# Up products of a ConvGLU feed-forward by one level of Strassen's algorithm, down products in pairs

## The chip, the cores and the metric

The kernel runs on one core of one Trainium2 chip. Its time is the device time of one launch in microseconds, the median of several runs. PE is TensorE, DVE is VectorE, ACT is ScalarE, POOL is GpSimd, and SP is SyncE, whose queue issues the transfers.

## The reference

One encoder layer runs over 2304 tokens of width 1024: 2048 of a sample and 256 of a prompt, with shared weights. After the mixers and the cross-attention comes the part that changes, and then the final norm:

```
a, g = split(rmsnorm(x) @ w_up)          # 1024 -> 2 x 2816: values a, gates g
g = conv over 3 neighbouring tokens of g, by channel, + bias
x = x + (silu(g) * a) @ w_down           # 2816 -> 1024
y = rmsnorm(x)
```

The convolution doesn't reach across the border of sample and prompt. Everything is float32.

## The kernel before

Products of float32 are made of two parts: hi is a value rounded to PE's format fp32r, lo the rest. `mm3` (lines 120 to 125) multiplies hi by hi, hi by lo and lo by hi into one PSUM tile. `load_split` (line 97) loads weights into a raw buffer, and ACT makes hi of them (line 116) and POOL lo (line 117).

`Ffn.run` works on three groups of 768 tokens (SG), each in two halves of 384 (TG). The 2816 inner features are 22 blocks f of 128. For each f, `up_part` loads the gates' and the values' weights and, half by half, adds 8 x 3 matmuls into `pg` (386 columns, the neighbours of the half with them) and 8 x 3 into `pa` (384 columns). Then comes the gate: ACT takes the middle tap of the convolution from `pg` (line 1958), DVE adds the outer two (line 1968), ACT makes tanh (line 1971), DVE two steps of the product (lines 1972 and 1973, the second with `pa`), ACT hi and POOL lo of the result u (lines 1975 and 1976).

`down_part` multiplies u of several f by their down weights: parts of 3, 3, 3, 3, 3, 3, 2, 2 blocks (PARTS). For each of 6 token blocks of 128 and each half of the 1024 outputs, 3 matmuls per f of 512 columns go into one `pd`, and DVE adds it to `acc` (line 1994). The last part also makes the output norm: a square on ACT (line 2000), a root on DVE, a scaling on ACT (line 2004), and a product with the weights of 1024 columns on POOL (line 2005).

`prep` makes the tokens of one half: it loads x, scales it by its norm (`rms_scale`, line 171), and transposes it on PE, and ACT and DVE make hi and lo of each transposed tile (`transpose_split`, lines 164 to 167), eight steps. `start` does this for the first half beside the last attention group, and the second is woven into the first up parts. For the next group it is woven into the last down parts.

PE's order is that of the code (`manual_schedule`). The order of the other engines' queues is made by the compiler's scheduler, which dispatches by readiness and, among ready ones, by the order of the code.

## Time and profile before

| | |
|---|---|
| median of 3 runs | 3730.86 us (3726.14 to 3733.28) |
| the profiled execution | 3726.75 us |
| its span | 3724.7 us |
| mean granted clock of PE | 0.981 |
| PE, DVE, ACT, POOL busy | 96%, 49%, 34%, 35% of the span |
| bytes moved | 340.37 MB, 91 GB/s on the mean |

The profile is one execution. Its span is what the engines' records cover, and the execution's own time is 2 us more. Durations of matmuls overlap, so what one costs is read from the distance of two starts.

### The profile page before, as it was taken

The numbers are of one execution on the slowest core, as the hardware profiler recorded it, in microseconds if no ns is written. First come the engines' busy times: TensorE is split into PE (matmuls) and PEld (weight loads), VectorE is DVE, ScalarE is ACT, GpSimd is POOL, SyncE is SP. The second block draws the span as 40 slices with busy tenths as digits, with TensorE's granted clock in tenths as the row PEclk, the third lists the DMA queues.
The fourth block names the chain that finished last, engine by engine and source line by source line (L and its number), as shares of the span: only waits on it lengthen the run. The fifth ranks groups of instructions, "written<-read, shape, count | busy, mean of one in ns | idle before, by whom it ended". The sixth has DMA issues, their size and how long they took to land.

```text
span 3724.7 us, 53214 instructions
## 1 busy us (share of the span) xinstructions
PE 3581.3 (96%) x20150; PEld 3084.8 (83%) x20150; DVE 1822.1 (49%) x4422; ACT 1275.4 (34%) x2632; POOL 1301.0 (35%) x1110
## 2 busy tenths in 40 slices
PE   7998999999899999999998999999999999999998
PEld 6998998898445555678887999988999998999997
DVE  5757777565653644355555333326333336333334
ACT  3321114453345445444444222224322224322222
POOL 3326435343345244200001433433423333433342
PEclk9999999999799999999998999999999999999999
DMA  6453443333141411312224212214211223211221
GB/s 209 165 190 110 164 151 105 108 125 83 44 122 45 118 38 27 129 52 75 74 74 154 74 52 68 74 62 134 87 52 57 68 75 101 87 57 52 63 80 51
DMA packets 212833, 340.37 MB, mean 91 GB/s; under 512 B 82913, under 2 KB 155105, under 8 KB 208353
## 3 DMA queue, kind: packets, MB, share of 16 engines
q1 hardware_dynamic: 212576, 336.97, 28.6%
q8 instruction: 159, 2.61, 0.3%
q14 instruction: 98, 0.79, 0.1%
HBM read 252.14 MB, written 84.77 MB: 90 GB/s over the span
## 4 chain that ended last, share of the span: by engine, by line
PE 83%; DVE 8%; DMA 3%; issue 2%; ACT 2%; POOL 1%; SPq 0%; ACTq 0%; DVEq 0%; POOLq 0%
PE pg L123 5%; PE pa L123 5%; PE pa L124 5%; PE pa L125 5%; PE pg L124 5%; PE pg L125 5%; PE pd L123 5%; PE pd L125 5%; PE pd L124 5%; PE po L1498 4%; PE mm L123 3%; PE mm L125 3%; PE mm L124 3%; PE ps L123 2%; PE pa L691 2%; PE ps L124 2%
## 5 line engine op out<-in xcount | busy, mean ns | idle before, releaser
L1968 DVE SCALAR_TENSOR_TENSOR gc<-pg,f_cw,gc 128x384 f32<-128x384 f32 (+4 forms) x308 | 166.5, 558 | 563.2 <-ACT gc L1958 559.4
L117 POOL TENSOR_TENSOR ul<-raw,uh 128x1024 fp32r<-128x1024 f32 x132 | 317.6, 2406 | 209.3 <-ACT uh L116 206.3
L123 PE MATMUL pg<-h,uh 128*128 128x386 f32 x1056 | 358.7, 340 | 0.9 <-DVE x L1809 0.9
L124 PE MATMUL pg<-h,uh 128*128 128x386 f32 x1056 | 357.6, 339 | 0.0
L125 PE MATMUL pg<-h,ul 128*128 128x386 f32 x1056 | 357.0, 338 | 0.0
L123 PE MATMUL pa<-h,uh 128*128 128x384 f32 x1056 | 356.9, 338 | 0.0
L124 PE MATMUL pa<-h,uh 128*128 128x384 f32 x1056 | 356.5, 338 | 0.0
L125 PE MATMUL pa<-h,ul 128*128 128x384 f32 x1056 | 356.3, 337 | 0.0
L1994 DVE TENSOR_TENSOR acc<-acc,pd 128x512 f32<-128x512 f32 x264 | 181.4, 687 | 312.9 <-PE pd L125 312.8
L123 PE MATMUL pd<-dh,uh 128*128 128x512 f32 x792 | 316.4, 399 | 8.1 <-DVE h L166 5.5
L1976 POOL TENSOR_TENSOR ul<-gc,uh 128x384 fp32r<-128x384 f32 x132 | 134.8, 1021 | 541.1 <-ACT uh L1975 541.1
L125 PE MATMUL pd<-dh,ul 128*128 128x512 f32 x792 | 313.8, 396 | 0.0
L124 PE MATMUL pd<-dl,uh 128*128 128x512 f32 x792 | 313.7, 396 | 0.0
L1481 POOL TENSOR_TENSOR sum<-sum,pe 128x512 f32<-128x512 f32 x168 | 214.2, 1284 | 194.6 <-ACT pe L1473 188.5
L117 POOL TENSOR_TENSOR dl<-raw,dh 128x1024 fp32r<-128x1024 f32 x66 | 158.8, 2406 | 265.1 <-ACT dh L116 265.1
L1958 ACT ACTIVATE gc<-pg,f_cw 128x384 f32<-128x384 f32 x132 | 87.2, 661 | 419.0 <-PE pg L125 415.8
L123 PE MATMUL mm<-wh,hhi 128*128 128x256 f32 x720 | 212.7, 295 | 4.6 <-DVE ut L363 4.0
L1473 ACT ACTIVATE pe<-ps 128x512 f32<-128x512 f32 (+1 forms) x264 | 151.0, 590 | 188.2 <-PE ps L1471 185.5
L123 PE MATMUL mm<-hhi,wh 128*128 128x384 f32 x576 | 208.0, 361 | 0.0
L1432 DVE TENSOR_REDUCE mx<-pm 128x1 f32<-128x512 f32 (+1 forms) x264 | 170.7, 678 | 72.0 <-PE pm L1429 70.9
L124 PE MATMUL mm<-wl,hhi 128*128 128x256 f32 x720 | 205.0, 285 | 0.0
L125 PE MATMUL mm<-wh,hlo 128*128 128x256 f32 x720 | 204.8, 284 | 0.0
(491 smaller groups left out, 8704.2 us busy)
## 6 DMA issues: line engine op xcount, KB each, us to landing
raw<-in_w_up SPq DMA_DIRECT2D x132, 512.0 KB
raw<-in_w_down SPq DMA_DIRECT2D x66, 512.0 KB
x<-in_x SPq DMA_DIRECT2D x36, 512.0 KB
hhi<-s_h SPq DMA_DIRECT2D x8, 1536.0 KB
hlo<-s_h SPq DMA_DIRECT2D x8, 1536.0 KB
raw<-in_w_in SPq DMA_DIRECT2D x22, 512.0 KB
s_h<-hhi SPq DMA_DIRECT2D x6, 1536.0 KB
s_h<-hlo SPq DMA_DIRECT2D x6, 1536.0 KB
```

The source lines that it names most:

```text
L117: (eng or nc.gpsimd).tensor_tensor(out=l, in0=raw, in1=f32(h), op=ALU.subtract)
L123: mm(out, lhsT=lh, rhs=rh, start=first, stop=False)
L124: mm(out, lhsT=lh, rhs=rl, start=False, stop=False)
L125: mm(out, lhsT=ll, rhs=rh, start=False, stop=last)
L1432: nc.vector.tensor_reduce(out=mx[:, qb, i:i + 1], in_=pm[:, :half], axis=AX.X, op=ALU.max)
L1473: nc.scalar.activation(out=pe[:, :nq], in_=ps[:, :nq], func=AF.Exp)
L1481: eng.tensor_tensor(out=t[:, :nq], in0=self.sums[h][:, :nq], in1=pe[:, :nq], op=ALU.add)
L1498: nc.tensor.matmul(po[hs, :nq], lhsT=va[:, vt, :], rhs=pe[:, :nq], start=kb == 0, stop=self.done)
L1958: nc.scalar.activation(out=gc, in_=pg[:, 1:TG + 1], func=AF.Identity, scale=cw[:, f, 1:2], bias=cw[:, f, 3:4])
L1968: V.scalar_tensor_tensor(out=gc[:, a:b], in0=pg[:, a + off:b + off], scalar=cw[:, f, tap:tap + 1], in1=gc[:, a:b], op0=ALU.mult, op1=ALU.add)
L1976: nc.gpsimd.tensor_tensor(out=ul[:, cs], in0=gc, in1=f32(uh)[:, cs], op=ALU.subtract)
L1994: V.tensor_tensor(out=acc[b][:, ns], in0=acc[b][:, ns], in1=pd, op=ALU.add)
```

## The change

The up products of one f become one 2 x 2 by 2 x 2 block product: rows are values and gates, the inner index the two halves of the 1024 features, columns the two token halves. One level of Strassen's algorithm (in Winograd's order) makes it with 7 products instead of 8. Product i multiplies weight operand i by token operand i, 4 x 3 matmuls of 386 columns each, and values, too, are made for the neighbours.

- `up_weights` makes seven weight operands of 512 columns per f from the raw weights: three are raw parts, four are sums or differences on DVE. `split` makes hi on ACT and lo on POOL (even operands) or DVE (odd ones). Their eight buffers are used in turn (`Slots`).
- `prep` makes seven token operands for each of 4 pairs of feature blocks, from four scaled tiles and four temporaries, for the whole group of 768. `start` makes two of the four pairs beside the last attention group; the other two follow in `run`.
- `up_part` adds the products in the PSUM tiles `px`, `py`, `pz`. Sums that can't be made there are made on DVE and ACT in SBUF tiles `y`, `z`, `v`: products 3, 5 and 6 continue the tile `px` after DVE or ACT has read it, and product 4 continues `pz`. Product 6 of f is computed after product 0 of f + 1.
- `gate` is the gate of before, now on `z` and `v` (second token half, both in SBUF) and on `px` and `y` (first half).
- Down products are made in pairs of f, in even f from 2 on, between products 2 to 5. Each tile takes 6 matmuls. The last pair of a group comes at the start of the next group, beside `prep`: six tiles ahead of it and two behind each of its steps. `pd` has two buffers instead of four.

```diff
-SG = 768
+SG = 2 * TG
 NSG = T // SG
 BSG = SG // P
-DOWN_FEW = 2
-PARTS = (3, 3, 3, 3, 3, 3, 2, 2)
+HC = TG + 2
+KH = KD // 2
+NP = 7
+DOWN_FROM = 2
...
+    def tile(self, dtype):
+        pool, tag = self.slots[self.at]
+        self.at = (self.at + 1) % len(self.slots)
+        return pool.tile([P, D], dtype, tag=tag, name=self.tag, bufs=1)
...
+        self.w = Slots(pool, "aw", 6)
+        self.raws = Slots(pool, "raw", 2)
+    def tokens(self, j):
+        return self.pool.tile([P, 2 * NP * HC], F32R, tag=f"h{j}", name=f"h{j}", bufs=1)
...
-        self.down = [Ring(wp, "d" + n, 4) for n in "hl"]
+        self.down = [Slots(wp, "d" + n, 2) for n in "hl"]
...
-        self.up = pool("u", 6, reuse_waits="tile")
-        self.ep = pool("e", 2, reuse_waits="tile")
+        self.up = pool("u", 3, reuse_waits="tile")
+        self.st = pool("t", 2, reuse_waits="tile")
+        self.ep = pool("e", 1, reuse_waits="tile")
         self.sm = pool("s", 2, reuse_waits="tile")
-        self.xp = pool("x", 2, reuse_waits="tile")
+        self.arena.w.add(wp, 2)
+        self.arena.raws.add(wp, 1)
         self.ps_u = pool("pu", 2, space=PSUM)
-        self.ps_d = pool("pd", 4, space=PSUM)
+        self.ps_d = pool("pd", 2, space=PSUM)
...
+        turn = itertools.cycle("xyz")
+        self.small = self.sm
+        self.turned = lambda shape: self.ps_u.tile(shape, F32, tag=next(turn), name="tr")
+        self.temps = lambda: [self.ep.tile([P, HC], F32, tag=t, name="tm", bufs=n) for t, n in
+                              (("y", 2), ("y", 2), ("z", 1), ("v", 1))]
+    def split(self, src, hi, lo, i):
+        nc = self.k.nc
+        nc.scalar.activation(out=hi, in_=src, func=AF.Copy)
+        (nc.vector if i % 2 else nc.gpsimd).tensor_tensor(out=lo, in0=src, in1=f32(hi), op=ALU.subtract)
...
+    def prep(self, sg, hs):
...
+        for b in range(BSG):
+            x = self.arena.w.tile(F32)
             nc.sync.dma_start(out=x, in_=s["x2"][t0 + b * P:t0 + (b + 1) * P, :])
             xs.append(x)
+        for n in range(2):
+            rms_scale(k, xs[BPG * n:BPG * n + BPG], xs[BPG * n:BPG * n + BPG], None, self.small, "fx",
+                      self.arena.raws.tile(F32))
+            yield 0
...
+        for j in range(KH):
+            h = self.tokens(j).rearrange("p (o s t) -> p o s t", o=NP, s=2)
+            hs.append(h)
+            turned = {}
+            for key in ((0, 0), (0, 1), (1, 1), (1, 0)):
+                kh, n = key
+                c = j + KH * kh
+                pt = self.turned([P, TG])
+                for b in range(BPG):
+                    nc.tensor.transpose(pt[:, b * P:(b + 1) * P], xs[BPG * n + b][:, c * P:(c + 1) * P], k.ident)
+                turned[key] = pt
+            def take(dst, key):
+                kh, n = key
+                c = j + KH * kh
+                nc.scalar.activation(out=dst[:, 1:TG + 1], in_=turned[key], func=AF.Copy, scale=fw[:, c:c + 1])
+                V.tensor_copy(dst[:, 0:HC:HC - 1], exs[n][:, c, :])
+            def op(i, src):
+                self.split(src, h[:, i, 0, :], h[:, i, 1, :], i)
+            def sub(out, x, y):
+                V.tensor_tensor(out=out, in0=x, in1=y, op=ALU.subtract)
+            ta, tb, tc_, td = self.temps()
+            take(ta, (0, 0))
+            take(tb, (0, 1))
+            take(tc_, (1, 1))
+            op(1, ta)
+            sub(td, tc_, tb)
+            op(5, td)
+            sub(tb, tb, ta)
+            op(2, tb)
+            sub(ta, tc_, tb)
+            op(3, ta)
+            op(4, tc_)
+            take(tc_, (1, 0))
+            op(0, tc_)
+            sub(tc_, tc_, ta)
+            op(6, tc_)
+            yield 1320
+    def up_weights(self, f, ops):
...
+        a, g = (arena.raws.tile(F32) for _ in range(2))
+        for raw, i in ((a, 0), (g, 1)):
+            nc.sync.dma_start(out=raw, in_=io["w_up"][f, i])
+        a1, a2, g1, g2 = a[:, :512], a[:, 512:], g[:, :512], g[:, 512:]
+        def op(src):
+            w = arena.w.tile(F32R)
+            self.split(src, w[:, :512], w[:, 512:], len(ops))
+            ops.append(w)
+        def comb(x, y, o):
+            t = self.st.tile([P, 512], F32, tag="st", name="st")
+            V.tensor_tensor(out=t, in0=x, in1=y, op=o)
+            return t
+        op(a2)
+        yield
+        op(a1)
+        yield
+        s1 = comb(g1, g2, ALU.add)
+        op(s1)
+        yield
+        s2 = comb(s1, a1, ALU.subtract)
+        op(s2)
+        yield
+        op(comb(a2, s2, ALU.subtract))
+        yield
+        op(comb(a1, g1, ALU.subtract))
+        yield
+        op(g2)
+        yield
+    def gate(self, f, pg, pa, u, q0, t0):
...
+        nc, ep, cw = self.k.nc, self.ep, self.cw
+        V = nc.vector
+        gc = ep.tile([P, TG], F32, tag="gc", name="gc", bufs=2)
...
+        V.scalar_tensor_tensor(out=gc, in0=th, scalar=1.0, in1=gc, op0=ALU.add, op1=ALU.mult)
+        V.scalar_tensor_tensor(out=gc, in0=gc, scalar=0.5, in1=pa[:, 1:TG + 1], op0=ALU.mult, op1=ALU.mult)
+        cs = slice(q0, q0 + TG)
+        nc.scalar.activation(out=u[:, 0, cs], in_=gc, func=AF.Copy)
+        nc.gpsimd.tensor_tensor(out=u[:, 1, cs], in0=gc, in1=f32(u)[:, 0, cs], op=ALU.subtract)
...
+    def up_part(self, f, ws, hs, us, t0, before):
+        k, nc, ep = self.k, self.k.nc, self.ep
+        V = nc.vector
+        def prod(i, ps, first=True, last=False):
+            for j in range(KH):
+                w = slice(j * P, (j + 1) * P)
+                wl = slice(512 + j * P, 512 + (j + 1) * P)
+                k.mm3(ps, ws[i][:, w], ws[i][:, wl], hs[j][:, i, 0, :], hs[j][:, i, 1, :],
+                      first and j == 0, last and j == KH - 1, i > 0)
+                yield i
+        def psum(t):
+            return self.ps_u.tile([P, HC], F32, tag=t, name="p" + t)
+        def tile(t, n=1):
+            return ep.tile([P, HC], F32, tag=t, name=t, bufs=n)
+        py, px, pz = psum("y"), psum("x"), psum("z")
+        yield from prod(0, py, last=True)
+        y = tile("y", 2)
+        nc.scalar.activation(out=y, in_=py, func=AF.Copy)
+        yield from before
+        yield from prod(1, px)
+        V.tensor_tensor(out=y, in0=px, in1=y, op=ALU.add)
+        yield from prod(2, pz)
+        z = tile("z")
+        nc.scalar.activation(out=z, in_=pz, func=AF.Copy)
+        yield from prod(3, px, False)
+        v = tile("v")
+        nc.scalar.activation(out=v, in_=px, func=AF.Copy)
+        yield from prod(4, pz, False, True)
+        V.tensor_tensor(out=v, in0=pz, in1=v, op=ALU.add)
+        yield from prod(5, px, False)
+        V.tensor_tensor(out=z, in0=px, in1=z, op=ALU.add)
+        u = self.up.tile([P, 2, SG], F32R, tag="u", name="u")
+        us.append(u)
+        self.gate(f, z, v, u, TG, t0)
+        def rest():
+            yield from prod(6, px, False, True)
+            self.gate(f, px, y, u, 0, t0)
+        return rest()
+    def down_weights(self, f):
+        hi, lo = (r.tile(F32R) for r in self.down)
+        drain(self.k.load_split(self.k.io["w_down"][f], hi, lo, self.arena.raws))
+        return hi, lo
+    def down_part(self, ws, us, acc, t0, last):
...
-        for b in blocks:
+        if last:
+            yw = self.arena.raws.tile(F32)
+            nc.sync.dma_start(out=yw, in_=io["norm_out"])
+        for i, b in enumerate((3, 4, 5, 0, 1, 2)):
             bs = slice(b * P, (b + 1) * P)
             for n in range(2):
                 ns = slice(512 * n, 512 * n + 512)
                 pd = self.ps_d.tile([P, 512], F32, tag="pd", name="pd")
-                for i in range(len(ws)):
-                    k.mm3(pd, us[i][0][:, bs], us[i][1][:, bs], ws[i][0][:, ns], ws[i][1][:, ns],
-                          i == 0, i == len(ws) - 1)
+                for j, (w, u) in enumerate(zip(ws, us)):
+                    k.mm3(pd, u[:, 0, bs], u[:, 1, bs], w[0][:, ns], w[1][:, ns], j == 0, j == len(ws) - 1)
                 V.tensor_tensor(out=acc[b][:, ns], in0=acc[b][:, ns], in1=pd, op=ALU.add)
-                yield 330
...
+                if n and last:
+                    x = acc[b]
+                    ss = sm.tile([P, 1], F32, tag="yss", name="yss")
+                    junk = self.up.tile([P, 2, SG], F32, tag="u", name="junk").rearrange("p s t -> p (s t)")[:, :D]
+                    nc.scalar.activation(out=junk, in_=x, func=AF.Square, accum_out=ss)
...
+                    if i < BSG - 1:
+                        nc.scalar.activation(out=x, in_=x, func=AF.Copy, scale=r[:, 0:1])
+                        nc.gpsimd.tensor_tensor(out=x, in0=x, in1=yw, op=ALU.mult)
...
+                yield
...
+        self.small = mid.sm
+        self.turned = lambda shape: mid.ps_t.tile(shape, F32, tag="tr", name="tr")
+        def temps():
+            ts = [self.arena.raws.tile(F32) for _ in range(2)]
+            return [t[:, c:c + HC] for t in ts for c in (0, 512)]
+        self.temps = temps
+        self.hs = []
+        self.ahead = self.prep(0, self.hs)
+        yield from itertools.islice(self.ahead, 8)
...
+            ops = []
+            first = self.up_weights(0, ops)
+            for _ in range(BSG):
+                next(downs, None)
+            for _ in ahead:
+                for _ in range(2):
+                    next(downs, None)
+            drain(first)
+            drain(downs)
...
+            us, ws = [], []
+            rest, downs, ahead, ahs = iter(()), iter(()), iter(()), []
+            for f in range(NF):
+                coming = []
+                if f + 1 < NF:
+                    beside_it = self.up_weights(f + 1, coming)
+                elif sg + 1 < NSG:
+                    ahead = self.prep(sg + 1, ahs)
+                    beside_it = itertools.islice(ahead, 4)
+                else:
+                    beside_it = iter(())
+                part = self.up_part(f, ops, hs, us, t0, rest)
+                at = done = 0
+                i0 = None
+                while True:
+                    try:
+                        i = next(part)
+                    except StopIteration as e:
+                        rest = e.value
+                        break
+                    if i != i0:
+                        next(beside_it, None)
+                        if f % 2 and i in (1, 4):
+                            ws.append(self.down_weights(f - (i == 1)))
+                        if f and f % 2 == 0 and i == DOWN_FROM:
+                            downs = self.down_part(ws[:2], us[:2], acc, t0, False)
+                            del ws[:2], us[:2]
+                        i0 = i
+                    if DOWN_FROM <= i < 6:
+                        at += 1
+                        while done < at * 2 * BSG // (4 * (6 - DOWN_FROM)):
+                            next(downs, None)
+                            done += 1
+                drain(downs)
+                drain(beside_it)
+                ops = coming
+            drain(rest)
+            downs = self.down_part(ws, us, acc, t0, True)
+            hs = ahs
+        drain(downs)
...
```

## Rows read from the trace of the kernel before

**Rows 1.** The page: busy us, share of the span and instructions of each engine.
```profile
PE 3581.3 (96%) x20150; PEld 3084.8 (83%) x20150; DVE 1822.1 (49%) x4422; ACT 1275.4 (34%) x2632; POOL 1301.0 (35%) x1110
```

**Rows 2.** Instructions of tile pg: count, min/median/max ns, first and last start us.
```profile
L123 PEld LDWEIGHTS pg<-h,uh x1056: 186/188/191, 2010.2 to 3673.8; 128*128 128x128 f32 x176
L123 PE MATMUL pg<-h,uh x1056: 335/339/425, 2010.2 to 3674.0; 128*128 128x386 f32 x176
```

**Rows 3.** Stretches: length, busy us (instructions) by engine, clock, DMA share, GB/s.
```profile
2130.00:2530.00 400.00, 400.00 (x2080) 373.09 (x2079) 133.94 (x189) 99.19 (x141) 147.27 (x79) 1.00 0.20 64
2530.00:2620.00 90.00, 83.88 (x430) 74.98 (x430) 63.31 (x198) 39.83 (x66) 28.24 (x15) 0.96 0.41 135
3080.00:3180.00 100.00, 96.25 (x516) 88.02 (x515) 58.64 (x188) 42.82 (x67) 37.25 (x21) 1.00 0.34 111
```

**Rows 4.** Timeline of PE: start us, duration us, line, operation, tiles, shapes.
```profile
2302.02 0.34 PE L123 MATMUL pg<-h,uh 128*128 128x386 f32 x1
...
2310.48 0.34 PE L123 MATMUL pg<-h,uh 128*128 128x386 f32 x1
...
2538.44 0.40 PE L123 MATMUL pd<-dh,uh 128*128 128x512 f32 x1
...
2539.61 0.39 PE L125 MATMUL pd<-dh,ul 128*128 128x512 f32 x1
```

**Rows 5.** Instructions of tile gc in 2130 to 2530 us.
```profile
L1968 DVE SCALAR_TENSOR_TENSOR gc<-pg,f_cw,gc x62: 617/618/621, 2146.8 to 2527.7; 128x384 f32<-128x384 f32 x62
L1958 ACT ACTIVATE gc<-pg,f_cw x31: 651/655/672, 2146.1 to 2526.3; 128x384 f32<-128x384 f32 x31
L1971 ACT ACTIVATE th<-gc x31: 507/525/527, 2148.2 to 2528.4; 128x384 f32<-128x384 f32 x31
L1972 DVE SCALAR_TENSOR_TENSOR gc<-th,gc x31: 557/559/2455, 2148.7 to 2528.9; 128x384 f32<-128x384 f32 x31
L1973 DVE SCALAR_TENSOR_TENSOR gc<-gc,pa x30: 553/555/556, 2150.2 to 2524.2; 128x384 f32<-128x384 f32 x30
L1975 ACT ACTIVATE uh<-gc x30: 504/524/527, 2150.8 to 2525.9; 128x384 fp32r<-128x384 f32 x30
L1976 POOL TENSOR_TENSOR ul<-gc,uh x30: 1006/1016/1024, 2151.4 to 2528.5; 128x384 fp32r<-128x384 f32 x30
```

**Rows 6.** Operands in SBUF alone, lines 1481 and 117: 512 and 1024 columns.
```profile
L1481 POOL TENSOR_TENSOR sum<-sum,pe x168: 1260/1275/1669, 968.9 to 1508.7; 128x512 f32<-128x512 f32 x168
...
L1481 DVE TENSOR_TENSOR sum<-sum,pe x56: 681/692/1669, 977.9 to 1508.2; 128x512 f32<-128x512 f32 x56
...
L117 POOL TENSOR_TENSOR dl<-raw,dh x66: 2393/2405/2425, 2090.8 to 3659.1; 128x1024 fp32r<-128x1024 f32 x66
```

**Rows 7.** ACT: a split of 1024 columns, a scaled copy of a transposed tile.
```profile
L116 ACT ACTIVATE dh<-raw x66: 1057/1059/1064, 2089.6 to 3658.0; 128x1024 fp32r<-128x1024 f32 x66
...
L165 ACT ACTIVATE h<-tr,f_nw x16: 562/582/586, 2546.5 to 2589.5; 128x384 fp32r<-128x384 f32 x16
```

**Rows 8.** Groups of DVE, 2130 to 2530 us: busy us, mean ns, idle before.
```profile
L1972 DVE SCALAR_TENSOR_TENSOR gc<-th,gc 128x384 f32<-128x384 f32 x31 | 33.5, 1082 | 26.4 <-ACT th L1971 26.4
```

**Rows 9.** Timeline of SP and ACT: a load of down weights and its split.
```profile
2162.15 7.42 SPq L114 DMA_DIRECT2D raw<-in_w_down  x2
...
2165.68 1.06 ACT L116 ACTIVATE dh<-raw 128x1024 fp32r<-128x1024 f32 x1 [1.99 <-DMA raw<-in_w_down]
```

**Rows 10.** Timeline of PE: three transposes and what follows.
```profile
2539.98 0.53 PE L164 MATMUL tr<-ident,x 128*128 128x128 f32 x3
2540.26 0.48 PE L123 MATMUL pd<-dh,uh 128*128 128x512 f32 x1
```

**Rows 11.** Timeline of PE: the first and last of 12 matmuls after a gap.
```profile
2569.07 0.77 PE L123 MATMUL pd<-dh,uh 128*128 128x512 f32 x1 [3.94 <-DVE h L166]
...
2573.90 0.63 PE L125 MATMUL pd<-dh,ul 128*128 128x512 f32 x1
```

More of the change, by code (lines that the diff above doesn't have):

```diff
@@ L118, in load_split, with mm3 @@
             yield
-    def mm3(self, out, lh, ll, rh, rl, first, last):
-        mm = self.nc.tensor.matmul
-        mm(out, lhsT=lh, rhs=rh, start=first, stop=False)
-        mm(out, lhsT=lh, rhs=rl, start=False, stop=False)
-        mm(out, lhsT=ll, rhs=rh, start=False, stop=last)
+    def mm3(self, out, lh, ll, rh, rl, first, last, partial=False):
+        for l, r, start, stop in ((lh, rh, first, False), (lh, rl, False, False), (ll, rh, False, last)):
+            self.nc.tensor.matmul(out, lhsT=l, rhs=r, start=start, stop=stop, skip_group_check=partial)
 def weave(main, filler):
@@ L1915, in prep @@
-        sm, ps, tag = self.small()
-        hi, lo = (h[:, i:i + KD * (TG + 2)].rearrange("p (k t) -> p k t", k=KD) for i in (0, KD * (TG + 2)))
-        pt = ps.tile([P, 2], F32, tag=tag, name="pe")
-        nc.tensor.matmul(pt, lhsT=self.ones, rhs=es, start=True, stop=True)
-        v = sm.tile([P, 2], F32, tag="fev", name="fev")
-        V.tensor_scalar(out=v, in0=pt, scalar1=1.0 / D, scalar2=EPS, op0=ALU.mult, op1=ALU.add)
-        r = k.rsqrt(sm, v, 2, "fe")
-        V.tensor_tensor(out=ex, in0=ex, in1=fw.unsqueeze(2).to_broadcast([P, KD, 2]), op=ALU.mult)
@@ L1979, in down_weights @@
-    def down_weights(self, fs):
-        return [self.weights(self.down, self.k.io["w_down"][f]) for f in fs]
-    def down_part(self, ws, us, acc, t0, last, blocks=range(BSG)):
+        exs = []
+        for n in range(2):
+            ex = self.arena.pool.tile([P, KD, 2], F32, tag="ex", name="ex", bufs=2)
+            for i, t in enumerate((max(t0 + n * TG - 1, 0), min(t0 + (n + 1) * TG, T - 1))):
+                nc.sync.dma_start(out=ex[:, :, i], in_=s["x2"][t].rearrange("(k p) -> p k", p=P))
+            exs.append(ex)
@@ new lines, in prep @@
+        yield 0
+        for n in range(2):
+            rms_scale(k, xs[BPG * n:BPG * n + BPG], xs[BPG * n:BPG * n + BPG], None, self.small, "fx",
+                      self.arena.raws.tile(F32))
+            yield 0
+        ess = []
+        for ex in exs:
+            sq = self.small.tile([P, KD, 2], F32, tag="esq", name="esq")
+            nc.scalar.activation(out=sq, in_=ex, func=AF.Square)
+            es = self.arena.pool.tile([P, 2], F32, tag="es", name="es", bufs=2)
+            V.tensor_reduce(out=es, in_=sq.rearrange("p k i -> p i k"), axis=AX.X, op=ALU.add)
+            ess.append(es)
@@ new lines, in prep @@
+        yield 0
+        for n, (ex, es) in enumerate(zip(exs, ess)):
+            pt = self.turned([P, 2])
+            nc.tensor.matmul(pt, lhsT=self.ones, rhs=es, start=True, stop=True)
+            v = self.small.tile([P, 2], F32, tag="fev", name="fev")
+            V.tensor_scalar(out=v, in0=pt, scalar1=1.0 / D, scalar2=EPS, op0=ALU.mult, op1=ALU.add)
+            r = k.rsqrt(self.small, v, 2, "fe")
+            V.tensor_tensor(out=ex, in0=ex, in1=fw.unsqueeze(2).to_broadcast([P, KD, 2]), op=ALU.mult)
+            V.tensor_tensor(out=ex, in0=ex, in1=r.unsqueeze(1).to_broadcast([P, KD, 2]), op=ALU.mult)
+            for cond, i in ((sg + n == 0, 0), (sg + n == NSG, 1)):
+                if cond:
+                    V.memset(ex[:, :, i:i + 1], 0.0)
+            yield 220
```

182 lines of the change are left out of this document (37 added, 145 removed).

## The prediction

> **What bounds the kernel now.** I read the busy shares first, then the feed-forward by stretches, then single instructions. TensorE (PE) is busy for 96% of the span [rows 1], so the question is what its time consists of. The feed-forward starts at 2010.2 us [rows 2] and runs to the end, 1714.5 us. In its steady stretch PE is busy 400.0 of 400 us at full granted clock, while DVE is busy a third of it, ACT a quarter and POOL 37% [rows 3]. Only the stretches around a change of token group show PE idle: 6.1 of 90 us and 3.8 of 100. So fewer matmuls shorten the stage exactly as long as the other three engines still deliver in time.
>
> What a matmul costs is its start-to-start distance, not its duration, because matmuls overlap. From one pg to the pg 48 matmuls later takes 8.46 us: 0.176 us each, for 386 and 384 columns alike. Five distances of pd take 1.17 us: 0.234 us for 512 columns [rows 4].
>
> **What is removed.** Before, one f takes 2 halves x 2 products x 8 x 3 = 96 matmuls, 6336 in all (three lines each for pg and pa, 1056 per line [rows 2]). After, 7 products P0 to P6 x 4 x 3 = 84, or 5544. So 792 x 0.176 = **-139.6 us**. The 18 x 2 x 22 x 3 = 2376 down matmuls stay. The Trainium skill ("TensorE: Matmul & The Clock Gate", Back-to-back issue gap) gives columns / 2.4 + 2.5, 163 ns here; the trace disagrees with 176, and by the page's figure the saving would be 129 us.
>
> **What is added per f.** PE order is P0(f), P6(f-1), P1 to P5, each 12 x 0.176 = 2.12 us. Down units (6 matmuls, 1.40 us) come only in even f, 12 of them among P2 to P5. An even f thus has 14.8 + 16.8 = 31.6 us of PE work, an odd one, which I call short, 14.8. There are 33 short ones.
>
> Each engine's work in a short f, from [rows 5 to 7], with 0.63 for an ACT copy of 512 columns, interpolated between 0.524 (384) and 1.06 (1024):
> - ACT: 7 weight halves 4.4, copies of y, z, v 1.6 (0.52 each, by 0.524 for 384 columns), two gates 2 x (0.66 + 0.52 + 0.52) = 3.4, two down weights 2.1: 11.5 us.
> - POOL: 4 x 1.28 + 2 x 1.02 + 2 x 2.41 = 12.0 us, 81%.
> - DVE: three lo parts and two sums of weights at 0.68 (two more sums need no free slot and can run in the long f before), three additions at 0.555, four taps and four gate steps at 0.55 to 0.62: 9.7 us.
>
> All are below 14.8, but DVE's is not its real time. gc<-th,gc, whose operands all lie in SBUF, takes 557 ns at least and 2455 at most, almost exactly one POOL instruction of 2.41 more; the DVE lines with a PSUM operand never pass 621 [rows 5, 6]. Its mean is 1082 [rows 8]: 0.52 us of waiting at a POOL share of 37%. Before, it is the only such line in the up part, two per f. After, 11 are in a short f: the weight work, both taps of the half whose z lies in SBUF, and the last gate step, which multiplied by PSUM and now by v or y.
>
> I scale the wait by POOL's share (81/37) and by the length of its instructions (the mean rest that one meets is 0.85 us after against 1.06 before, weighted by length): 0.52 x 2.2 x 0.8 = 0.91 us per line. What this does to PE, two ways:
> - By the chain. P3 adds into px, so it waits until DVE has read px for y. If DVE keeps the order of the code, gate(f-1) stands ahead of that. From the end of P6(f-1): 0.66 (gc) + 1.24 (taps) + 0.52 (th) + 0.56 + 0.55 + 0.555 (y) = 4.1 us; P3 is due at 4.23. There is no slack, and two of these lines wait for POOL: 1.8 us.
> - By throughput. DVE needs 9.7 + 11 waits; stretched over 18 us the POOL share falls and a wait is 0.75, so 17.9 us: 3.1 beyond 14.8. Behind DVE, ACT is held too (uh waits for the gate), and the copies of z and v that P4 and P5 wait for are queued there.
>
> I take the middle, 2.5 us x 33 = **+82 us**. The bounds are 0 (the scheduler puts the additions first and the waits fall into slack) and the sum of what POOL and DVE do on SBUF alone, 12.0 + 8.1 = 20.1 us, 5.3 beyond PE. In even f the same chain has three down units (4.2 us) in each gap and costs nothing; without them it would cost as in the short ones. SP issues the same transfers as before. The latest is the second down weight: its raw buffer comes free when a1 - g1 is formed, about 11 us into the short f (after P2's slot and two lines each on ACT and DVE); from request to copy took 3.5 us [rows 9], then 1.1 and 2.4 for its halves: 18 us, and the first unit that reads it comes 7 us into the even f, at 22. Hidden, unless POOL is 4 us behind.
>
> **What moves: the tokens.** Before, 8 steps of ACT and DVE per half are woven between matmuls. After, each of the four steps j of prep makes seven operands through four temporaries with one buffer each, so the next step waits for the last subtraction of this one. Its longest path: take 1.7 (3 x 0.58), copy 0.52, POOL lo 1.02, take 0.58, copy 0.52, POOL lo 1.02, subtraction 0.55, copy 0.52, POOL lo 1.02 [rows 5, 7]: the period is 7.5 us if ACT runs the ready copy of op 4 early, 9.4 with handovers if POOL does op 2 first. I take 8.5, and 6.4 until op 0 of the last step, which P0 needs.
>
> *Change of token group, twice.* After P5 of the last f, the additions and gate 1 take 5.5 us to the last u, covered by P6 and three matmuls (2.8): 2.7 idle. The 12 last units now stand beside prep, but ten of them ahead of its first transposes, so they hide only its loads and norms. Then 3 x 8.5 + 6.4 = 31.9 us, in which PE has two units (2.8) and 48 transposes (three end within 0.28 us, 0.093 each [rows 10]: 4.5): 24.6 idle, plus one output norm's 128x1024 piece on POOL, 2.4 [rows 6], that stands in its way. After the idle time PE restarts slowly: following a gap of 3.94 us, 12 matmuls of 512 columns ran 0.44 apart [rows 11], the lower level, 1.2 GHz; 12 x (0.44 - 0.234) = 2.4 us. Sum 32.1. Before, the two changes cost 6.1 + 2.4 and 3.8 [rows 3, 11]. 2 x 32.1 - 12.3 = **+52 us**.
>
> *Start.* Steps j = 2, 3 stand alone after the last attention group: 8.5 + 6.4 - 24 transposes (2.2) + 2.4 = +15. Steps 0 and 1 stand in that group's PE order, with four transposed tiles from three PSUM buffers and temporaries from the ring that the attention also uses. The trace has nothing like it; I bound it by 0 (hidden by that group's own waits) and 15 (two full steps), and take 6, nearer to 0, since the group has waits to hide it in. **+21**. *End.* The late u of the last f: **+3**. Output norms that wait for a scratch buffer of u could add up to 10 at each of three ends; I take none, because each needs its buffer only for 1 us.
>
> **Sum.** -139.6 + 82 + 52 + 21 + 3 = +18.4, about 19. The profiled execution took 3726.75 us (span 3724.7 and 2 around it), the median run 3730.86, 4 above. So 3746 for such an execution and **3750** for the median.
>
> **Rivals.**
> - *The waits fall into slack: faster.* If DVE's order puts the additions of y and z ahead of the gate's tail, a short f loses 0.5 us at most (16 in all): 3730.9 - 139.6 + 16 + 76 = 3683. It decides at (139.6 - 76) / 33 = 1.9 us per short f. For it: the additions have PSUM operands, which never wait, and weight work has most of an f until it is due. Against it: the 4.1 of 4.23 us.
> - *The port is the bound: much slower.* If POOL and DVE exclude each other completely on SBUF, a short f lasts 20.1 us: 5.3 x 33 = 175, giving 3730.9 - 139.6 + 175 + 76 = 3842. For it: the maximum of 2455. Against it: POOL's last pieces can run on into the long f. The Trainium skill ("SBUF — State Buffer", SBUF: two separate sides) states this as an exclusive lock held for a whole instruction; the trace agrees with its 557 and 2455.
> - *Prep is hidden after all.* If the scheduler overlaps the steps so that changes and start cost 30 instead of 73, with 2.5 us per short f: 3706. Against it: single buffers.
> - *The removed matmuls do not save.* Weight loads take 188 ns each, more than 176 [rows 2]. But each matmul has its own load, before and after, so loads fall by the same eighth. Without the saving: 3889; I give this 2%.
>
> **Chances.** Forecast 0.52 (own range 3715 to 3790; within it, 0.08 for no measurable change, which is 0.2% or 7 us); slack 0.28; port 0.12; prep hidden 0.06; no saving 0.02. Faster: 0.28 + 0.06 + 0.03 from the low edge of the forecast = 0.37; same 0.08; slower 0.55. The bounds reach from 3650 (no waits, steps at 7.5, attention 0) to 3890 (port, steps at 9.4, late norms); leaving out 2 in 10: 3665 to 3845.
>
> **What would show it.** Right: 5544 up matmuls at 0.176; gc<-th,gc and the lo lines on DVE well above their minimum, in odd f only; PE waiting there for DVE at px (P3, P6) and for ACT at P4, P5, some 2.5 us per odd f; two idle stretches of about 25 us with ACT, POOL and DVE taking turns, and one of about 13 after the attention. Wrong: PE dense in odd f (then 3683), or odd f of 20 us; steps j that overlap; a start of the feed-forward much after 2016.

## The result and the profile after

The changed kernel takes 4013.5 us (4000.2 to 4019.9 over four runs), against 3728.5 us for the kernel before, measured beside it: a ratio of 1.076, with an interval of 1.073 to 1.079. It is slower, as forecast, but by 285 us where the prediction had 19, and far outside its range of 3665 to 3845. The profiled execution took 4011.6 us, its span 4009.3.

From the page of the changed kernel: the busy line of the engines, and from the costliest groups the three PSUM tiles of the seven products.

```profile
PE 3577.5 (89%) x19358; PEld 3031.0 (76%) x19358; DVE 2428.8 (61%) x5288; ACT 1521.4 (38%) x3244; POOL 1430.4 (36%) x1286
...
L124 PE MATMUL px<-h,aw 128*128 128x386 f32 x3168 | 656.2, 356 | 68.5 <-ACT v L2088 55.0
...
L124 PE MATMUL pz<-h,aw 128*128 128x386 f32 x1584 | 322.8, 340 | 2.6 <-ACT z L2085 2.6
...
L124 PE MATMUL py<-h,aw 128*128 128x386 f32 x792 | 170.3, 366 | 53.2 <-ACT h L1903 25.5
```

The 792 matmuls are gone: 20150 [rows 1] became 19358, and 3168 + 1584 + 792 are the 5544 foreseen. But PE, busy for 96% before, is busy for 89% of a longer span. The windows say where: the steady stretch, a long (even) f inside it, and the first change of token group. The columns are the stretch, its length, busy time of PE, weight loads, DVE, ACT and POOL, granted clock, DMA share and GB/s.

```profile
2130.00:2530.00 400.00, 357.98 (x1740) 324.68 (x1741) 239.54 (x349) 137.03 (x249) 151.63 (x103) 0.96 0.20 60
...
2299.60:2337.70 38.10, 33.93 (x158) 29.52 (x157) 24.39 (x34) 10.49 (x19) 11.09 (x8) 0.96 0.16 47
2600.00:2745.00 145.00, 92.47 (x427) 80.82 (x426) 106.11 (x259) 68.56 (x125) 61.06 (x41) 0.79 0.32 106
```

Where PE was busy for 400.00 of 400 us [rows 3], it now idles for 42, and at the change for 53 of 145, with the mean clock at 0.79. What PE waited for in the feed-forward, in us in total, times, and the longest:

```profile
PE pd L124 <- DVE acc L2123: 89.9, 36, 3.6
PE px L124 <- ACT v L2088: 55.0, 30, 2.0
PE tr L1962 <- ACT tm L1968: 42.6, 10, 8.5
PE py L124 <- ACT h L1903: 25.5, 4, 8.4
PE py L124 <- ACT tm L1968: 25.4, 3, 8.6
PE pd L124 <- ACT u L2053: 19.5, 19, 2.0
```

The largest wait is one that the prediction doesn't have: a down unit waits for a pd buffer, which DVE has not yet added to acc.

I measure each f from the start of its P0 to that of the next. "Change" is the last f of a group, its last down units and prep, up to the next group's P0. The forecast column follows from the prediction's own terms: for a change 14.8 + 2.5 for the last f, 2.1 for its P6, 16.8 for twelve units, 4.5 for transposes, 32.1 idle; for f = 0, 6 x 2.12.

| Piece | forecast, us | measured, us | missing in all, us |
|---|---|---|---|
| 30 long f (even, 2 to 20) | 31.6 | 37.48 (35.6 to 39.5) | 176 |
| 2 changes, and f = 0 after each | 72.8 + 12.7 | 91.8 + 26.0 | 65 |
| start: first P0, and its f = 0 | 2031.2; 12.7 | 2035.2; 27.1 | 18 |
| 30 short f (odd, 1 to 19) | 17.3 | 17.46 (16.7 to 18.6) | 5 |

They sum to 264 of the 266 us between the forecast for a profiled execution (3746) and the measured one. Two thirds stand in the f that I had called free. Of those 176 us, PE's waits in the 30 long f make 101; the rest is matmuls that ran further apart.

First a short f, just before the long one that follows, by the timeline of all engines (start, duration, engine, line, operation, idle time before and its releaser):

```profile
2292.74 1.30 POOL L1904 TENSOR_TENSOR aw<-st,aw 128x512 fp32r<-128x512 f32 x1
...
2294.08 0.69 DVE L2011 TENSOR_TENSOR st<-raw,st 128x512 f32<-128x512 f32 x1 [2.91 <-POOL aw L1904]
2294.69 0.55 DVE L2050 SCALAR_TENSOR_TENSOR gc<-th,gc 128x384 f32<-128x384 f32 x1
...
2295.87 0.52 ACT L2053 ACTIVATE u<-gc 128x384 fp32r<-128x384 f32 x1 [3.17 <-DVE gc L2051]
...
2296.82 0.47 ACT L2088 ACTIVATE v<-px 128x386 f32<-128x386 f32 x1
...
2297.34 2.38 PE L124 MATMUL px<-h,aw 128*128 128x386 f32 x12 [1.85 <-ACT v L2088]
```

No DVE line is stretched here. DVE stands idle for 2.91 us ahead of the third sum of weights: the sums have two buffers `st`, and POOL must first have read the one that this sum overwrites. The gate stands behind the sum in DVE's queue, the copy to v behind the gate's u in ACT's, and P5 waits 1.85 us for v. Such a wait comes twice in each short f. From the waits of all engines in the feed-forward:

```profile
DVE st L2011 <- POOL aw L1904: 200.1, 89, 2.9
```

146 of these us fall in the 30 short f. All DVE lines there exceed the shortest of their kind by 13 us in sum, in the 30 long f by 135 us: the stretched lines are a matter of the long f.

The long f after it:

```profile
2299.32 0.69 DVE L2011 TENSOR_TENSOR st<-raw 128x512 f32<-128x512 f32 x1 [2.15 <-POOL aw L1904]
...
2299.57 2.29 PE L124 MATMUL py<-h,aw 128*128 128x386 f32 x12
...
2301.96 2.39 POOL L117 TENSOR_TENSOR dl<-raw,dh 128x1024 fp32r<-128x1024 f32 x1 [2.67 <-ACT dh L116]
...
2303.03 3.31 DVE L2046 SCALAR_TENSOR_TENSOR gc<-z,f_cw,gc 128x384 f32<-128x384 f32 x2 [1.49 <-ACT gc L2036]
2304.31 1.62 POOL L1904 TENSOR_TENSOR aw<-raw,aw 128x512 fp32r<-128x512 f32 x1
...
2308.18 0.52 ACT L2053 ACTIVATE u<-gc 128x384 fp32r<-128x384 f32 x1 [0.65 <-DVE gc L2051]
...
2308.75 0.51 PE L124 MATMUL pd<-dh,u 128*128 128x512 f32 x1 [0.86 <-ACT u L2053]
...
2309.84 0.50 PE L124 MATMUL pd<-dh,u 128*128 128x512 f32 x1 [0.35 <-POOL u L2054]
...
2312.51 1.57 POOL L1904 TENSOR_TENSOR aw<-st,aw 128x512 fp32r<-128x512 f32 x1
2312.88 1.61 DVE L2050 SCALAR_TENSOR_TENSOR gc<-th,gc 128x384 f32<-128x384 f32 x1
2314.53 0.56 DVE L2051 SCALAR_TENSOR_TENSOR gc<-gc,y 128x384 f32<-128x384 f32 x1
2315.00 0.68 DVE L2123 TENSOR_TENSOR acc<-acc,pd 128x512 f32<-128x512 f32 x1
...
2315.74 0.51 PE L124 MATMUL pd<-dh,u 128*128 128x512 f32 x1 [2.96 <-DVE acc L2123]
...
2317.07 0.63 PE L124 MATMUL pd<-dl,u 128*128 128x512 f32 x1
...
2317.49 0.63 PE L124 MATMUL pd<-dh,u 128*128 128x512 f32 x1
...
2337.65 2.29 PE L124 MATMUL py<-h,aw 128*128 128x386 f32 x12
```

Read it from the top. DVE has stood 2.15 us for an `st` buffer, so the additions ahead of the first gate are late. While POOL makes the low part of a down weight (2301.96 to 2304.35) and then one of an up weight (to 2305.93), DVE starts the gate's two taps; they take 3.31 us instead of 2 x 0.61. So tanh and u come late, and the first unit, due in this f, waits 0.86 and 0.35 us for u. DVE then works off what is queued (a th line that again takes 1.61 us beside POOL's 1.57), and only at 2315.00 adds the first pd to acc. Both pd buffers are full until then, and the third unit waits 2.96 us. Soon after it PE runs at the lower of its two clock levels (1.2 of 2.4 GHz; the mean granted clock of these 3.7 us is 0.54): pd 0.42 us apart against 0.234 [rows 4].

```profile
2316.30:2320.00 3.70, 3.70 (x12) 3.30 (x11) 2.70 (x4) 0.24 (x1) 0.86 (x1) 0.54 0.11 17
```

This f takes 38.08 us, 6.5 more than 31.6: 4.17 of waiting and 2.3 of matmuls further apart. By the distances in the timeline some 1.5 of the 2.3 are from the lower clock; the rest is spread over the restarts after each wait and the other matmuls.

The lines of gc and acc on DVE in 2130 to 2530 us (min/median/max ns) show which are stretched:

```profile
L2046 DVE SCALAR_TENSOR_TENSOR gc<-z,f_cw,gc x30: 610/1524/1761, 2138.2 to 2524.7; 128x384 f32<-128x384 f32 x30
L2046 DVE SCALAR_TENSOR_TENSOR gc<-px,f_cw,gc x30: 606/614/620, 2143.2 to 2528.6; 128x384 f32<-128x384 f32 x30
...
L2050 DVE SCALAR_TENSOR_TENSOR gc<-th,gc x29: 550/559/1615, 2142.1 to 2526.9; 128x384 f32<-128x384 f32 x29
...
L2123 DVE TENSOR_TENSOR acc<-acc,pd x84: 679/687/690, 2149.8 to 2502.7; 128x512 f32<-128x512 f32 x84
```

The same tap never passes 620 ns with px in PSUM and reaches 1761 with z in SBUF. The addition that PE waits for is itself never slow (690 at most); it is late, because it stands behind instructions that are.

### The profile page after: what moved, and what is told of

Its sections match the earlier page's. It is cut to its first block, busy times and chain, and to the rows that moved or that the text cites. A ratio compares the mean times of both kernels' runs of the same rounds, so it can differ in the third digit from the quotient of the medians.

```text
span 4009.3 us, 53281 instructions
## 1 busy us (share of the span) xinstructions
PE 3577.5 (89%) x19358; PEld 3031.0 (76%) x19358; DVE 2428.8 (61%) x5288; ACT 1521.4 (38%) x3244; POOL 1430.4 (36%) x1286
## 4 chain that ended last, share of the span: by engine, by line
PE 40%; issue 18%; DVE 16%; POOL 10%; DMA 10%; ACT 4%; SPq 1%; POOLq 0%; ACTq 0%; DVEq 0%
PE mm L124 9%; PE ps L124 7%; POOL aw L1904 5%; DMA raw<-in_w_down 4%; PE po L1497 3%; DMA raw<-in_w_up 3%; PE pa L690 2%; POOL dl L117 2%; PE ps L1469 2%; POOL u L2054 2%; PE pd L124 2%; PE px L124 1%; PE ps L1470 1%; DVE st L2011 1%; PE pm L1428 1%
## 5 line engine op out<-in xcount | busy, mean ns | idle before, releaser
L124 PE MATMUL px<-h,aw 128*128 128x386 f32 x3168 | 656.2, 356 | 68.5 <-ACT v L2088 55.0
L124 PE MATMUL pd<-dh,u 128*128 128x512 f32 x1584 | 598.7, 420 | 119.0 <-DVE acc L2123 89.9
L124 PEld LDWEIGHTS px<-h,aw 128*128 128x128 f32 x3168 | 600.7, 201 | 98.4 <-ACT v L2088 64.5
L124 PEld LDWEIGHTS pd<-dh,u 128*128 128x128 f32 x1584 | 315.6, 199 | 209.4 <-DVE acc L2123 101.8
L1904 POOL TENSOR_TENSOR aw<-raw,aw 128x512 fp32r<-128x512 f32 x132 | 183.1, 1387 | 437.2 <-ACT aw L1903 421.3
L124 PE MATMUL pd<-dl,u 128*128 128x512 f32 x792 | 325.9, 412 | 0.0
L124 PE MATMUL pz<-h,aw 128*128 128x386 f32 x1584 | 322.8, 340 | 2.6 <-ACT z L2085 2.6
L124 PEld LDWEIGHTS pz<-h,aw 128*128 128x128 f32 x1584 | 286.9, 190 | 14.9 <-ACT z L2085 3.3
L1904 POOL TENSOR_TENSOR aw<-st,aw 128x512 fp32r<-128x512 f32 x132 | 182.4, 1382 | 243.4 <-ACT aw L1903 241.5
L124 PE MATMUL py<-h,aw 128*128 128x386 f32 x792 | 170.3, 366 | 53.2 <-ACT h L1903 25.5
```

The costliest lines, as they stand in the source:

```text
L124: self.nc.tensor.matmul(out, lhsT=l, rhs=r, start=start, stop=stop, skip_group_check=partial)
L1904: (nc.vector if i % 2 else nc.gpsimd).tensor_tensor(out=lo, in0=src, in1=f32(hi), op=ALU.subtract)
```

## Experiments

Two suspects stood against each other for the long f: DVE held up by POOL, and the order and buffers of the down units. (The diff also halves the pd buffers, from four to two; the prediction gives that no term.) All experiments compute the full result, and each is the changed kernel with the edit shown, but for the pairs alone, which start from the kernel before, and the last three, each of which adds its edit to the run before it.

**Down units later.**
```diff
-DOWN_FROM = 2
+DOWN_FROM = 4
```


> The twelve down units of an even f spread over P4 and P5 instead of P2 to P5. Theory (order): the units start before the last half of u exists, and their additions then stand in DVE's queue behind the gate and weight work, so two pd buffers hold PE up; started 4.2 us later they meet a finished u. Long f falls from 37.5 us to 33 to 35, the time from 4013 to 3880 to 3940, and short f stay at 17.5. Rival (DVE is full): the additions are slow because DVE waits for the port, wherever they stand; twelve in two products instead of four crowd it more: long f 37 to 39, time 4000 to 4060.

Measured: 3994 us, ratio 1.072 (1.069 to 1.074). Long f 38.6 us, short f 15.9. The rival had the long f; the time fits neither side. The main wait of the feed-forward became another:

```profile
PE px L124 <- DVE y L2082: 116.1, 48, 6.0
...
PE pd L124 <- DVE acc L2123: 37.1, 33, 2.4
```

The units no longer wait so much (37 us against 90), but without them in its gaps P3 waits for y, which DVE adds late as well. Moving the units is no cure: in this place, too, what comes first in an even f meets a late DVE. The short f got 1.5 us shorter because P5's waits for v fell from 55.0 us to 10.1 in sum; why the other engines were earlier there is not taken apart.

**Low parts on DVE.**
```diff
-            self.split(src, w[:, :512], w[:, 512:], len(ops))
+            self.split(src, w[:, :512], w[:, 512:], 1)
...
-        nc.gpsimd.tensor_tensor(out=u[:, 1, cs], in0=gc, in1=f32(u)[:, 0, cs], op=ALU.subtract)
+        nc.vector.tensor_tensor(out=u[:, 1, cs], in0=gc, in1=f32(u)[:, 0, cs], op=ALU.subtract)
...
-        drain(self.k.load_split(self.k.io["w_down"][f], hi, lo, self.arena.raws))
+        drain(self.k.load_split(self.k.io["w_down"][f], hi, lo, self.arena.raws, self.k.nc.vector))
```


> All low parts of the steady stretch (up weights, down weights, u) on DVE, none on POOL; the tokens' preparation is as it was. Theory (waits for POOL): without POOL every DVE line on SBUF alone falls to its minimum (gc<-z from a mean of 1.10 us to about 0.56, sums from 0.80 to 0.56). DVE's work per pair of f rises to about 38 us of 46.4, which it can do: short f 16 to 17 us, long f 33 to 35, time 3850 to 3920. Rival (DVE's amount of work is the bound): about 15.4 us of work against 14.8 of PE in a short f, so short f become 19 or more, long f stay at 37, time 4013 to 4100.

Measured: 3802 us, ratio 1.020 (1.018 to 1.022), 212 less than the changed kernel and 48 below the range of the theory. Long f 32.46, short f 16.04. DVE has more instructions and is done sooner. Its tap on z in 2130 to 2570 us:

```profile
L2046 DVE SCALAR_TENSOR_TENSOR gc<-z,f_cw,gc x36: 609/618/620, 2159.1 to 2566.8; 128x384 f32<-128x384 f32 x36
```

and in the windows, 2130 to 2530 us, PE 387.99 busy with DVE at 314.92 and POOL at 0:

```profile
2130.00:2530.00 400.00, 387.99 (x1983) 356.48 (x1982) 314.92 (x516) 158.00 (x282) 0.00 (x0) 1.00 0.20 65
```

DVE at 79% with nothing beside it keeps PE better supplied than DVE at 60% beside POOL at 38%. So the amount of work was not the bound; the waits for POOL were. They are of two kinds, and this run removes both: the stretched lines (in the long f from 135 us to 11 beyond their shortest), and DVE's waits for `st` (from 200 us to none). What each alone costs PE no run shows; more `st` buffers with POOL left as it was would tell.

The Trainium skill ("SBUF — State Buffer", Who interferes with whom) says that a DVE instruction with two SBUF inputs contends with a GpSimd instruction that reads SBUF, and that the one that issued second is blocked until the first finishes. The trace agrees for the stretched lines: 1761 ns at most beside POOL, 620 without it.

**A third pd buffer**, taken from the y tiles, which then have one.
```diff
-        self.ps_d = pool("pd", 2, space=PSUM)
+        self.ps_d = pool("pd", 3, space=PSUM)
...
-            return self.ps_u.tile([P, HC], F32, tag=t, name="p" + t)
+            return self.ps_u.tile([P, HC], F32, tag=t, name="p" + t, bufs=1 if t == "y" else 2)
```
(The transposed tiles of tag y get one buffer in the same way.)

> A third PSUM buffer for pd, taken from py, which then has one. Theory (order): PE waits 90 us in all for DVE's additions before a pd; a third buffer lets a unit more go ahead, but the units still start before u and the additions still come late, so only a part returns: 3960 to 4000, long f 36 to 37. Rival (the two buffers are the cause): nearly all of the 90 us returns, time 3910 to 3940, long f 34.5 or less. If py with one buffer costs, it shows in py waiting for ACT at P0.

Measured: 3896 us, ratio 1.045 (1.043 to 1.047), 118 less, 100 of them in the long f. Long f 34.13, short f 17.27. In the waits, acc fell from 89.9 to 17.0, but the waits for u rose from 19.5 to 30.8:

```profile
PE pd L124 <- ACT u L2053: 30.8, 25, 2.9
PE pd L124 <- DVE acc L2123: 17.0, 21, 1.9
```

The time is below both ranges, and the rival, the two buffers as a cause, came nearer than my theory. But with a buffer free the units still wait for a late u.

**The pairs alone**, in the kernel before.
```diff
-PARTS = (3, 3, 3, 3, 3, 3, 2, 2)
+PARTS = (2,) * 11
```


> The kernel before with its down products in eleven pairs instead of six groups of three and two pairs; the up products are plain. Theory: the pairs alone cost nothing that can be measured, 36 additions of 0.69 us more per token group on an idle DVE, within 7 us of 3728. Rival: every group of down units waits for its last u, so three more groups per token group cost 3 us each, 3750 to 3760, and the pairs would then be part of the slowdown.

Measured: 3728.1 us against 3729.1, ratio 1.0001 (0.9991 to 1.0010). As the theory had it, pairs cost nothing, with four pd buffers and plain up products.

**Both cures.** Low parts on DVE and three pd buffers, the edits above together.

> Low parts on DVE and a third pd buffer together; alone they gave back 212 and 118 us. Theory (one cause, two cures): the late additions come from DVE waiting for POOL, and the third buffer only lets PE run over them; so the two overlap: long f 31.8 to 32.3 us (ideal 31.6), time 3770 to 3795. Rival (two causes that add up): 3802 - 118 = 3684, below the kernel before.

Measured: 3760 us, ratio 1.0083 (1.006 to 1.011): the theory's side, and a little better than its range in the long f and, by 10 us, in the time. Long f 31.54 (31.50 to 31.56), short f 16.00. Here is a whole long f with no gap, its window, and the start of the next:

```profile
2259.29 2.29 PE L124 MATMUL py<-h,aw 128*128 128x386 f32 x12
...
2290.83 0.34 PE L124 MATMUL py<-h,aw 128*128 128x386 f32 x1
```
```profile
2259.20:2290.80 31.60, 31.60 (x158) 28.50 (x157) 23.69 (x39) 10.76 (x19) 0.00 (x0) 1.00 0.15 51
```

With 31.54 as the floor, the four kernels split the long f's excess: POOL back with three buffers 2.59 us (78 in 30 f), two buffers without POOL 0.92 (28), both together 5.94 (178). So 72 us belong to neither alone: a late DVE hurts more when there is less buffer to run ahead on.

**Only the down weights' low parts on DVE.** The third edit of "Low parts on DVE" by itself.

> Only the low parts of the down weights (two of 2.41 us per short f, 40% of POOL's 12.0 us) move to DVE; up weights and u stay on POOL. If DVE waits for the rest of the POOL instruction that it meets, long pieces count by the square of their length (2 x 2.41^2 of 20.2 in all, 57%): some 120 of the 212 us return, time 3880 to 3905. Rival (POOL's share alone counts): 40%, 85 us, 3925 to 3935. If DVE gets too much (2.2 us more per short f): over 3960.

Measured: 3905 us, ratio 1.048 (1.046 to 1.050), 108 less: half of the 212, nearer to the count by squares (120) than by share (85), at the edge of its range. Short f fell to 15.59 and long f to 35.87 only. But the trace does not show the squares at work. In the short f, which give more than half of the gain, the stretched lines hardly change (13 us to 12); DVE's waits for `st` fall from 146 us to 106, as POOL no longer has the long pieces in its queue ahead of those that free the buffers (in the short f shown, one of 2.41 us). In the long f the stretched lines fall from 135 us to 96, by 29% and not 57%.

**The output norm on DVE.**
```diff
-                    if i < BSG - 1:
+                    if False:
```


> The output norm's scaling by ACT and its product with the norm's weights by POOL (2.41 us each, five per token group) replaced by the one DVE instruction (1.28 us) that the last block has already. Theory (POOL blocks DVE at the change too): small DVE instructions of the tokens' preparation wait 2.2 us behind each of the products; changes shrink by 6 to 12 us each, time 3990 to 4002, the products P0 to P6 as they were. Rival (the steps of prep are bound by their own chain of temporaries): no change, 4008 to 4018.

Measured: 3986 us, ratio 1.069 (1.067 to 1.071), 27 less; more than the theory, though the changes shrank by 5.8 and 5.1 us only; the end shrank by 8.7. In the changed kernel, two of POOL's products and the DVE instructions that started beside them, at the first change:

```profile
2665.67 2.38 POOL L2133 TENSOR_TENSOR acc<-acc,raw 128x1024 f32<-128x1024 f32 x1 [2.42 <-ACT acc L2132]
...
2678.52 2.35 POOL L2133 TENSOR_TENSOR acc<-acc,raw 128x1024 f32<-128x1024 f32 x1 [2.75 <-ACT acc L2132]
```
```profile
2660.88 0.16 DVE L1948 TENSOR_TENSOR ex<-ex,fe_y 128x16 f32<-128x16 f32 x1
...
2665.72 2.36 DVE L1948 TENSOR_TENSOR ex<-ex,fe_y 128x16 f32<-128x16 f32 x1
...
2678.66 2.22 DVE L93 TENSOR_TENSOR fy_t<-fy_t,fy_h 128x1 f32<-128x1 f32 x1
```

An instruction on 16 columns that took 0.16 us a moment earlier takes 2.36. Such lines form the chain of the norm's root, and prep's first step stands in the same queue: from its first scaled copy to that of the second step 18.1 us, and 10.3 in this run, which took away POOL's products and ACT's scalings together.

**Units among the steps of prep.**
```diff
-            for _ in range(BSG):
-                next(downs, None)
-            for _ in ahead:
-                for _ in range(2):
+            for n, _ in enumerate(ahead):
+                for _ in range(2 if n < 3 else 3):
                     next(downs, None)
```


> Of the twelve last down units of a token group, four stand ahead of the first transposes of the next one, two behind step 0 and three behind each of steps 1 and 2, instead of ten ahead and two behind. Theory (PE's order): prep starts six units (8.4 us) earlier and the units fill its gaps; each change shrinks by 6 to 10 us, time 3992 to 4002. Rival (prep competes with the output norms on ACT, DVE and POOL): the norms end later and stand in the way of the later steps; 4005 to 4030.

Measured: 3988 us, ratio 1.070 (1.068 to 1.072), 25 less, a little more than the theory; the changes shrank by 5.3 and 6.4 us, the end and the steady f by most of the rest. Prep starts earlier, but its steps now take 14.9, 16.7 and 18.8 us instead of 18.1, 12.8 and 13.8, with the norms among them. Both sides are right in part.

**All four edits.**

> Low parts on DVE, third pd buffer, norm on DVE and units among the steps, all together: 3760 with the first two. Theory (the last two act at different places of the change, POOL's products on the late steps and the units on the early ones): -27 and -25 nearly add up, 3705 to 3720, faster than the kernel before. Rival (both shorten the same wait): 3730 to 3740, no faster than before.

Measured: 3730.3 us, ratio 1.000 (0.999 to 1.001). From 3760 the norm and the units give 30 us together and not 52, the sum that the rival had. Its reason, one wait that both shorten, is not what the pieces show: the changes shrank by 11.3 and 13.1 us, as much as by the two edits alone added up (11.1 and 11.6). What is missing is mainly elsewhere: the first P0 came 4.5 us later and not 3.5 earlier, the end gave 7.8 and not 11.2, and the short f, which had given 10.6, gave 0.4.

**The tokens' low parts on DVE too.**
```diff
-                self.split(src, h[:, i, 0, :], h[:, i, 1, :], i)
+                self.split(src, h[:, i, 0, :], h[:, i, 1, :], 1)
```


> As the run with all four, and the tokens' low parts on DVE too, so POOL has nothing in the feed-forward. A step of prep is then 7.4 us of DVE (7 low parts and 4 subtractions of 0.56, 8 small copies) and 6.0 of ACT. Theory (waits for POOL lengthen the steps, 8.9 us apart now): steps 7.5 apart, 1.4 less in each of four steps at two changes and two at the start: 10 to 16 us less than the run with all four. Rival (DVE was the bound of the steps anyway, POOL took a third of it off): no change or up to 10 us more.

Measured: 3722.2 us, ratio 0.9979 (0.9970 to 0.9987), 8 less, between the two sides. Steps at the first change are 9.8, 10.2 and 11.2 us apart, not 7.5; in the run with all four they were 11.7, 12.0 and 10.9, not the 8.9 that I had written. So POOL was only a part of what sets their distance; what the rest is, no run here takes apart.

**Two buffers for the temporaries z and v.**
```diff
-            ... (("y", 2), ("y", 2), ("z", 1), ("v", 1))]
+            ... (("y", 2), ("y", 2), ("z", 2), ("v", 2))]
```
(The tiles z and v of `up_part`, which share these tags, get two as well.)

> As the run before, with two buffers each for the temporaries z and v, so that a step of prep need not wait for the last subtractions of the step before it. Theory (each step waits for its temporaries, as predicted): steps overlap and their distance falls to what DVE needs; 5 to 15 us less than the run before. Rival (DVE is busy all through the steps): within 4 us of it.

Measured: 3719.2 us, ratio 0.9965 (0.9952 to 0.9979). 3 us less than the run before is within the scatter of either (3708 to 3725 and 3715 to 3728), and the changes take 76.2 us in both: the temporaries, by which the prediction explained the steps, hardly bind.

**P0's operand made second in the last step.**
```diff
+            last = j == KH - 1
-            for key in ((0, 0), (0, 1), (1, 1), (1, 0)):
+            for key in ((0, 0), (1, 0), (0, 1), (1, 1)) if last else ((0, 0), (0, 1), (1, 1), (1, 0)):
...
             take(ta, (0, 0))
+            if last:
+                take(td, (1, 0))
+                op(0, td)
...
-            op(0, tc_)
+            if not last:
+                op(0, tc_)
```


> As the run with two buffers for z and v; in the last step of prep the operand of P0 is made second instead of sixth, since PE waits 8 to 10.5 us for it at each of three places. Theory (P0 alone is late: the other operands come in the order of the products, one in less than 2 us): the waits before P0 fall to about 5 us, 3 x 5 us less, 3700 to 3708, at most 0.994 of before. Rival (the whole last step is late): the wait moves to P2 and P3, whose operands go through the same chain; 3714 to 3720, no gain over the run before.

Measured: 3708.2 us (3701.4 to 3712.8) against 3727.7, ratio 0.9944 (0.9929 to 0.9959). This one beats the kernel before, by 0.56%. Its waits, where the run before had 28.9 us in 3 for py and 23.1 in 28 for y:

```profile
PE px L124 <- DVE y L2087: 34.4, 32, 6.4
...
PE py L124 <- ACT tm L1969: 5.3, 3, 2.8
```

Changes fell from 76 to 67 us, but f = 0 after them rose from 14.8 to 25 and 21, where P3 waits for y (12 of the 34.4 us; the rest is in short f). In this profile the move gains next to nothing at the changes: half of the theory, and then the rival. The time is at the edge of the theory's range (3700 to 3708). The interval of its ratio overlaps that of the run before, so whether this last edit gains anything stays open; that the sum of the edits does is shown.

## Why the prediction was wrong

**The step that failed** is "in even f the same chain has three down units (4.2 us) in each gap and costs nothing". It cost 5.9 us in each of 30 long f, 176 us. PE waits there for pd buffers that DVE has not emptied (79 us) and for u (22), and runs more slowly after the waits. I took the units as work that PE has at hand. But a unit needs the u that the late gate makes, and a pd buffer that the same late DVE must empty; two were left of four. The cover hung on what it was to cover. With POOL off DVE's back and a third buffer the step is true: 31.54 us, all PE.

**The short f came out by luck.** The term of 2.5 us was near the mark: 17.46 us by 17.3. But its mechanism, eleven lines on SBUF alone that wait 0.75 to 0.91 us each for POOL, makes 8 to 10 us in a short f, and the stretched lines measure 0.44. In their place DVE stood 4.9 us in each short f for two `st` buffers that POOL had yet to read, a wait for which the prediction has no term. Of the two ways that it averaged, P3 waited for y in no short f; PE's one wait in each is P5's for v, 1.83 us, with ACT held behind DVE as the second way has it. The first way appears only without POOL: with both cures P3 waits for y 24.8 us in 30 short f, which stay at 16.0.

**The port is real, but it acts in the long f.** There lines on SBUF alone take up to 1761 ns beside POOL, the same tap with a PSUM operand stays at 620, and without POOL all fall to their minimum. "In odd f only" was wrong: the gate that is late in an odd f runs in the even one, where it meets POOL's weight work. The rival "port is the bound" gave 20.1 us for a short f, which no f took (18.6 at most). Its 8.1 us of DVE also count the two taps on px, which have a PSUM operand; the eleven lines alone make 6.9, and 18.9 us in all.

**The saving came in full**: 5544 matmuls at 0.176 to 0.178 us where nothing holds them up, and a long f at 31.54 against 31.6 worked out.

**The changes** were mis-sized, 65 us missing in two. Steps of 8.5, 8.5 and 8.5 us measured 18.1, 12.8 and 13.8, and from the last step's first copy until P0 went on with its last operand it took 13.0 and not 6.4: 57.6 us by 31.9. The norm, of which one piece of 2.4 us was counted, cost step 0 7.8 us, by the run that takes it off POOL and ACT; the lock on DVE shown there is a part of this. I explained late norms by a scratch buffer, and "I take none" stood on the wrong reason. I also let P0 start when its last operand was due, but it started and then waited inside:

```profile
2705.96 2.62 PE L124 MATMUL py<-h,aw 128*128 128x386 f32 x7 [8.39 <-ACT tm L1968]
...
2718.34 0.69 PE L124 MATMUL py<-h,aw 128*128 128x386 f32 x1 [8.40 <-ACT h L1903]
```

So f = 0 took 26.0 us instead of 12.7. With one y buffer (the third pd run) f = 0 takes 14.2 to 15.2 and the change 99: mostly the same wait, moved ahead of P0 (114 us for the two together against 118).

**The start** missed 4 us to P0 and 14 inside its f = 0, of the same kind; no run took it apart. P0's start differed from 2032 to 2045 us between the kernels, and why stays open. **The end** and **the pairs** were as forecast, within the 2 us that are left and by the run of the pairs alone.

## What to carry to other kernels

Before a stall is called covered, ask what the covering work itself needs: operands and buffers that come from the late engine cover nothing. Where POOL works beside DVE, ask for two waits: DVE lines on SBUF alone that meet a POOL instruction, and buffers that DVE is to write and POOL has yet to read, with all that stands behind them in DVE's queue. Moving POOL's work to a busier DVE took 212 of 285 us off here. And every buffer count that a diff lowers needs a term of its own: two pd buffers instead of three cost 28 us in the long f with a punctual DVE and 100 with a late one. A term that comes out right is no proof of its mechanism: the short f had the size forecast, from another wait.

## What the hardware showed that was not expected

DVE instructions on 1 to 16 columns take as long as the POOL instruction beside them: 2.22 and 2.36 us instead of some 0.16. And a wait of 2.96 us was followed by matmuls at the lower clock level; in the long f shown, 2.3 us of matmuls further apart came on top of 4.17 us of waiting.
